# Decay rows through DRAM, side-by-side gate weights and one table load in a two-layer attention and delta-rule trunk

## The chip, the cores and the metric

One core of a Trainium2 chip runs the whole program. The metric is the device time of one execution, in microseconds; less is better. Four engines compute (TensorE, called PE in the profile, with its weight loads as PEld; VectorE, DVE; ScalarE, ACT; GpSimd, POOL), and SP only issues transfers.

## What is computed

A token sequence `x` of 256 by 2048 goes through two layers. Layer 0 is differential attention and a gated MLP with a short convolution (the FFN). Layer 1 is a gated delta rule (GDN) and the same kind of FFN. The change touches the beginning of layer 1 only:

```python
h = rms_norm(x, mixer_norm[1])
proj = h @ w_in                      # q, k, v, z and, last, b_gate and a_gate: 32 heads each
q, k, v = silu(causal_dwconv(...));  q, k = l2_norm(q), l2_norm(k)
beta = sigmoid(b_gate)
g = -exp(a_log) * softplus(a_gate + dt_bias)
g_c = cumsum(g)                      # within chunks of 64 in the reference
decay = exp(where(tril, g_c[:, None] - g_c[None, :], -inf))
low = where(strict, (k * beta) @ k.T * decay, 0);  qk = where(tril, q @ k.T * decay, 0)
```

So for every value head `h` the kernel needs a matrix whose element (i, j) depends on `g_c[i] - g_c[j]`: one of the two is a column (a scalar per partition), the other a row that must stand on all 128 partitions.

## The kernel before, in words

Activations live transposed: 128 features on partitions, 256 tokens along the row, in fp32 split into a high part (`fp32r`) and the rest. Every dense layer streams its weights. `weights()` (lines 78 to 91) loads one chunk `raw` of four 128-row blocks by 256 columns (512 KB) on SP's queue, ACT casts it to `whi` (line 89), and DVE subtracts for `wlo` (line 90). `dense()` (101) then makes three products per block and output tile, hi by hi, lo by hi, hi by lo (lines 115 to 117), 24 in a full chunk. `raw`, `whi` and `wlo` have three buffers each. After each chunk `tick()` (73) advances every generator in the list `bg` by one `yield`: all other work of a layer is written as such generators, and so is spread between the dense chunks.

This gives the program's order. The framework then orders each engine's instructions by a timeline that it simulates: what isn't ready there is passed by what is, and the result is fixed at build time. Each engine, and SP with its transfers, works through its own list in order.

In `gdn()` (409), the norm of layer 1 (`norm_stat`, 165) and the gates go first. `norm_stat` sums the squares by products with ones (177, 179), then `Ln` and `Exp` on ACT (182, 183). The gate weights are padded from 64 to 128 columns, and `dense` makes 16 x 3 products of them (664). `gates()` (704) scales the result (712), transposes it by two products with an identity (716), computes beta and the decays, their running sums by products with `triu` (744 to 752), and leaves a column tile `col` (negative sums by partition) and `rows`: 32 rows of sums in a high part and, 32 partitions below, the rest.

Then come four batches of four key heads. For each key head, `keys()` (455) makes for its two value heads a 128 x 128 matrix `sel` with ones in two rows (470, POOL, from the table `hot`), and a product of `sel` with `rows` (472) puts that head's row on all 128 partitions of a PSUM bank `gb`. DVE adds column and mask (475), ACT takes `Exp` (485 and 486, the latter from `gb` directly), in one block with the `Ln` and `Exp` of the l2 norm (480 to 482); a table set with both `ln` and `exp` is loaded for the block by `lnexp()` (189). SiLU (452) needs another table. PSUM has four `mp` banks for all such work. After the heads of a batch come its value heads, output gates `z` (dense_tok, 125) and, one batch later, the output products (`out`, 659), whose activations lie in the tile `oc`.

`HP`, `AP`, `OP`, `GAP` and `LEAD` (lines 23, 24) place the weight tiles in SBUF relative to the activations they meet, in elements modulo 128.

Of the kernel before, what the change touches and what calls it, by code (L numbers as in the profile page):

```python
# [3 lines left out]

# [12 lines left out]
P = 128  # L17
T = 256
# [9 lines left out]
class Trunk:  # L28
# [92 lines left out]
    def merge(self, ps, u):  # L121

        self.nc.vector.tensor_tensor(u, ps[:, :, :T], self.rstd.unsqueeze(1).to_broadcast([P, 2, T]), ALU.mult)  # L123

    def dense_tok(self, w, kt, acts):

        nc = self.nc
        ps = self.banks()
        for k0, nk in self.chunks(kt, CK // 2):
            hi, lo = self.weights(w[:, k0:k0 + nk, :], HP + LEAD)  # L130
            for k in range(nk):
                a = acts(k0 + k)
                first, last = k0 + k == 0, k0 + k == kt - 1
                for c in range(2):
                    ah, al = (a[:, i, c * P:(c + 1) * P] for i in range(2))
                    for j, (l, r) in enumerate(((ah, hi), (ah, lo), (al, hi))):
                        nc.tensor.matmul(ps[:, c, :], l, r[:, k, :], start=first and not j, stop=last and j == 2)  # L137
            self.tick()
        return ps
# [22 lines left out]
            nc.vector.tensor_tensor(self.ss, self.ss, sq, ALU.add)  # L162
        self.squares = []

    def norm_stat(self, wait=1):

        nc = self.nc
        r = self.sp.tile([P, T + 2], F32, tag="rstd", name="rstd", bufs=1)
        self.rstd, self.rstdc = r[:, :T], r[:, T:]
        for _ in range(wait):  # L170
            yield
        self.add_squares()
        yield
        self.add_squares()
        ss, self.ss = self.ss, None
        ps = self.mp()
        nc.tensor.matmul(ps[:, :T], self.ones, ss, start=True, stop=True)
        for c in range(2):
            nc.tensor.matmul(ps[:, T + c:T + c + 1], ss[:, c * P:(c + 1) * P], self.ones[:, :1], start=True, stop=True)
        m = self.sp.tile([P, T + 2], F32, tag="sq", name="ms", bufs=2)  # L180
        nc.vector.tensor_scalar(m, ps[:, :T + 2], 1.0 / D, EPS, ALU.mult, ALU.add)
        nc.scalar.activation(r, m, AF.Ln)
        nc.scalar.activation(r, r, AF.Exp, scale=-0.5)
        nc.vector.tensor_tensor(m, m, r, ALU.mult)
        nc.vector.tensor_tensor(m, m, r, ALU.mult)
        nc.vector.tensor_scalar(m, m, -0.5, 1.5, ALU.mult, ALU.add)
        nc.vector.tensor_tensor(r, r, m, ALU.mult)
# [218 lines left out]
            self.tick()  # L406
        return items[k]

    def gdn(self, w_gate, w_in, w_z, w_out, nb, hb, gate_ap, const_ap, hot_ap, conv_col, ng, done):

# [7 lines left out]
        gh = min(2, hb)  # L420
        gv = 2 * gh
        with tc.tile_pool(name="gd", bufs=1) as gd:
            self.spawn(self.norm_stat())
            con = gd.tile([P, 384], F32, tag="con", name="con")[:, :384]
            nc.sync.dma_start(con, const_ap)
            ident, mask, triu = con[:, :P], con[:, P:T], con[:, T:]
            hot = gd.tile([P, nv], F32, tag="hot", name="hot")
            nc.sync.dma_start(hot, hot_ap)
            gp = gd.tile([P, 2, nv], F32, tag="gp", name="gp")
            nc.sync.dma_start(gp, gate_ap)  # L430
            eps128 = gd.tile([P, 1], F32, tag="eps128", name="eps128")
# [23 lines left out]
            def keys(hq, c, cc, b0, res):  # L455
# [2 lines left out]
                nc.scalar.square(sq, c)  # L458
                sp = gd.tile([P, 2, 2, T], F32R, tag="qp", name="qp", bufs=1)
                self.split(sp, sq)  # L460
                yield
                yield
                while "rows" not in gates:
                    yield
                gb, gc = mp(), gates["col"]
                ds = []
                for v in range(2):
                    h = 2 * hq + v
                    sel = gd.tile([P, P], F32R, tag="sel", name="sel", bufs=2)
                    nc.gpsimd.tensor_copy(sel, hot[:, h:h + 1].to_broadcast([P, P]))  # L470
                    g = gb[:, v * T:(v + 1) * T]
                    nc.tensor.matmul(g, sel, gates["rows"], start=True, stop=True)
                    d = gd.tile([P, 384], F32, tag="d", name="d", bufs=2)
                    for t in range(2):
                        nc.vector.scalar_tensor_tensor(
                            d[:, (1 - t) * P:(2 - t) * P], g[:, t * P:(t + 1) * P], gc[:, t, h:h + 1], mask, ALU.add, ALU.add)
                    ds.append(d)
# [183 lines left out]
                    ps = self.dense(w_out[b * (KD // 2) + blk], 2 * hb, lambda k: self.await_(acts, k), OP)  # L661
                    self.add_out(blk, ps, done if b == nb - 1 else None)

            pg = self.dense(w_gate, KD, self.h_acts, HP, tiles=1)
            self.spawn(self.gates(gd, pg, nv, gp, ident, triu, gates))
            pend = None
            for b in range(nb):
                heads = range(b * hb, (b + 1) * hb)
# [32 lines left out]
                pend = (b, acts)  # L701
            out(*pend)

    def gates(self, gd, pg, nv, gp, ident, triu, res):

        nc, mp = self.nc, self.mp
        t0 = gd.tile([P, 4, 2, 64], F32, tag="vz", name="gt0", bufs=4)
# [5 lines left out]
        yield  # L713
        pt = mp()[:, :4 * nv].rearrange("p (t h) -> p t h", t=2)
        for t in range(2):
            nc.tensor.transpose(pt[:, t, :], lin[:2 * nv, t * P:(t + 1) * P], ident[:2 * nv, :2 * nv])
        for t in range(2):
            nc.vector.tensor_scalar(y[:, t, :nv], pt[:, t, :nv], -1.0, None, ALU.mult)
            nc.vector.tensor_tensor(y[:, t, nv:], pt[:, t, nv:], gp[:, 1, :], ALU.add)
# [10 lines left out]
        nc.vector.tensor_scalar(y, y, 0.0, None, ALU.max)  # L730
        nc.vector.scalar_tensor_tensor(q, q, 2.0, y, ALU.mult, ALU.add)
        a = gd.tile([P, nv], F32, tag="ga", name="ga")
        nc.scalar.activation(a, gp[:, 0, :], AF.Exp)
        if nv < 32:
            nc.vector.memset(w, 0.0)
        for t in range(2):
            for d in range(2):
                nc.vector.scalar_tensor_tensor(
                    w[:, t, 32 * d:32 * d + nv], q[:, t, nv:], -1.0, a, ALU.mult, ALU.mult)
        yield  # L740
        yield
        yield
# [3 lines left out]
        nc.tensor.matmul(pc[:, 1, :], self.ones, w[:, 0, :nv], start=False, stop=True)  # L746
        col = gd.tile([P, 2, nv], F32, tag="gc", name="gc")
        nc.vector.scalar_tensor_tensor(col, pc, -1.0, q[:, :, :nv], ALU.mult, ALU.subtract)
        pr = mp()[:64, :T]
        nc.tensor.matmul(pr[:, :P], w[:, 0, :], triu, start=True, stop=True)  # L750
        nc.tensor.matmul(pr[:, P:], w[:, 0, :], self.ones, start=True, stop=False)
        nc.tensor.matmul(pr[:, P:], w[:, 1, :], triu, start=False, stop=True)
        rows = gd.tile([P, T], F32R, tag="grow", name="grow")
        nc.gpsimd.memset(rows[64:].bitcast(F32), 0.0)
        nc.scalar.copy(rows[:64], pr)
        nc.vector.tensor_tensor(rows[32:64], pr[32:], rows[32:64].bitcast(F32), ALU.subtract)
        res["rows"], res["col"] = rows, col


NH = 8  # L760
# [11 lines left out]
def _layout(inputs):  # L772
# [30 lines left out]
    for t, n in ((0, P), (1, T)):  # L803
# [18 lines left out]
        "fcols1": fcols[1],  # L822
        "w_up0": blocks(x["ffn_w_up"][0], KD, up),
        "w_down0": blocks(x["ffn_w_down"][0], NJ, pairs(D // T)),
        "w_gate": np.pad(wi[:, 2 * kd + 2 * vd:], ((0, 0), (0, P - 2 * NV))).reshape(KD, P, P).transpose(1, 0, 2),
        "w_in": blocks(wi, KD, gin),
        "w_z": blocks(wi, KD, gz),
        "w_out": go.reshape(NB * (D // T), P, 2 * HB, T),
        "gate": np.broadcast_to(np.stack([x["gdn_A_log"][0], x["gdn_dt_bias"][0]]), (P, 2, NV)),
        "const": np.concatenate(const, 1).astype(f),  # L830
        "hot": np.concatenate([np.eye(NV)] * 2 + [np.zeros((P - 2 * NV, NV))]).astype(f),
        "w_up1": blocks(x["ffn_w_up"][1], KD, up),
        "w_down1": blocks(x["ffn_w_down"][1], NJ, pairs(D // T)),
    }
# [3 lines left out]
def trunk_kernel(tc, a, out):  # L838
    nc = tc.nc
    with ExitStack() as ctx:  # L840
        t = Trunk(ctx, tc)
        n = a["cols"].shape[1]
        cols = t.cp.tile([P, n], F32, tag="cols", name="cols")
        nc.sync.dma_start(cols[:, :KD], a["cols"][:, :KD])
        parts = t.chunks(KD, CK, 1)

        def load():
            if parts:
                k, n = parts.pop(0)
                nc.scalar.dma_start(t.x[:, k:k + n, :], a["x"][:, k:k + n, :])  # L850

        load()
        pos = [0]

        def take(n):
            pos[0] += n
            return cols[:, pos[0] - n:pos[0]]

        def one(c, i):
            return c[:, i:i + 1]  # L860

        mixer, ffn = take(2 * KD), take(2 * KD)
        qg, kg, lvec, sub, ng = take(1), take(1), take(4), take(2), take(1)
        gconv = take(4 * 4 * NQ)
        def then(gain, layer):
            return lambda k: t.norm_tile(k, one(gain, layer * KD + k))

        starts = [k for k, _ in parts]
        begun = []

        def start(k):

            if len(begun) <= k:
                if k == 0 or k in starts:
                    load()
                if k == KD - 1:
                    nc.scalar.dma_start(cols[:, KD:], a["cols"][:, KD:])
                then(mixer, 0)(k)
                t.add_squares()
                begun.append(k)  # L880
            return t.h[k]

        t.attention(a["w_qk"], a["w_v"], a["w_o"], NH, a["dist"], a["const"][:, :P], qg, kg, lvec, sub, start, then(ffn, 0),
                    0.8 - 0.6 * math.exp(-0.3 * 0))
        t.ffn(a["w_up0"], a["w_down0"], NJ, a["fcols0"], then(mixer, 1))
        t.gdn(a["w_gate"], a["w_in"], a["w_z"], a["w_out"], NB, HB, a["gate"], a["const"], a["hot"],
              lambda tap, tile_: one(gconv, tap * 4 * NQ + tile_), ng, then(ffn, 1))
        t.ffn(a["w_up1"], a["w_down1"], NJ, a["fcols1"],
              lambda k: nc.sync.dma_start(out[:, k, :], t.x[:, k, :]), final=True)
# [15 lines left out]
```

## Time and profile before

| | us |
|---|---|
| device time, median of 3 runs | 2651.64 |
| lowest and highest | 2649.69, 2652.61 |
| the profiled execution, device time | 2653.89 |
| its span in the profile | 2652.1 |
| TensorE, DVE, ACT, POOL busy in it | 2635.5, 1842.5, 1452.8, 110.9 |

Busy time of an engine is the time in which at least one of its instructions runs. Matmuls overlap, so their mean durations are latencies, and the distance between two starts is the pace. The granted TensorE clock is shown as a share of full speed (2.4 GHz; the other level is 1.2 GHz). The part of layer 1 before its FFN runs from about 1104 to 1910 us of the span.

### The profile page before, as it was taken

What the parts mean: (1) busy time and instruction counts of PE and PEld (TensorE: products, weight loads), DVE (VectorE), ACT (ScalarE), POOL (GpSimd) and SP (SyncE); (2) the same over time, 40 slices, a digit from 0 to 9 for tenths busy, and PEclk for the clock granted to TensorE, in tenths of its full rate; (3) what the DMA queues carried; (4) which work ended last, traced back from release to release, by engine and by line L of the source; (5) the groups of instructions that cost most, each with busy time, mean ns of one, the idle gap of its engine ahead of it and who ended that gap; (6) DMA issues with size and microseconds to landing.
All of it is one profiled execution on the core that took longest, in us unless ns stands there. A gap on an engine that the chain in (4) does not pass through costs nothing.

```text
span 2652.1 us, 53671 instructions
## 1 busy us (share of the span) xinstructions
PE 2635.5 (99%) x22352; PEld 2573.5 (97%) x22352; DVE 1842.5 (69%) x2719; ACT 1452.8 (55%) x1994; POOL 110.9 (4%) x221
## 2 busy tenths in 40 slices
PE   8999999999999999999999999999999999999999
PEld 8998899999999999999989989989999999999999
DVE  7776567777777555589788688688677777775444
ACT  6555555555555444485664674574555555554333
POOL 0000000000000000021011021021000000000000
PEclk9999999999999999999999999999999999999999
DMA  6555566666666666656455455555466666666665
GB/s 201 172 177 167 166 193 194 196 193 194 195 193 196 191 196 195 185 157 189 128 167 168 146 169 164 158 167 177 147 193 195 192 195 194 193 196 196 202 202 166
DMA packets 135460, 481.62 MB, mean 182 GB/s; under 512 B 15408, under 2 KB 18480, under 8 KB 135216
## 3 DMA queue, kind: packets, MB, share of 16 engines
q1 hardware_dynamic: 134064, 475.58, 60.1%
q8 instruction: 175, 2.87, 0.5%
q10 hardware_dynamic: 1152, 2.61, 0.3%
q14 instruction: 69, 0.57, 0.1%
HBM read 476.03 MB, written 2.10 MB: 180 GB/s over the span
## 4 chain that ended last, share of the span: by engine, by line
PE 96%; ACT 2%; DVE 2%; issue 1%; DMA 0%; SPq 0%; DVEq 0%; ACTq 0%
PE ps L116 27%; PE ps L115 27%; PE ps L117 27%; PE ps L137 10%; PE mp L607 2%; PE mp L223 1%; DVE wlo L90 0%; ACT whi L89 0%; PE mp L495 0%; PE mp L577 0%; PE mp L571 0%; DVE cv L204 0%; PE mp L586 0%; DMA raw<-w_qk 0%; PE mp L651 0%
## 5 line engine op out<-in xcount | busy, mean ns | idle before, releaser
L90 DVE TENSOR_TENSOR wlo<-raw,whi 128x1024 fp32r<-128x1024 f32 (+2 forms) x909 | 1105.9, 1218 | 638.8 <-ACT whi L89 636.8
L89 ACT CAST whi<-raw 128x1024 fp32r<-128x1024 f32 (+2 forms) x909 | 948.2, 1044 | 1011.8 <-PE ps L117 839.4
L115 PE MATMUL ps<-h,whi 128*128 128x256 f32 x4304 | 1193.6, 278 | 8.9 <-ACT h L149 5.6
L116 PE MATMUL ps<-h,wlo 128*128 128x256 f32 x4304 | 1194.0, 277 | 3.1 <-DVE wlo L90 3.1
L117 PE MATMUL ps<-h,whi 128*128 128x256 f32 x4304 | 1192.7, 277 | 0.0
L115 PEld LDWEIGHTS ps<-h,whi 128*128 128x128 f32 x4304 | 809.8, 188 | 11.0 <-ACT h L149 5.6
L116 PEld LDWEIGHTS ps<-h,wlo 128*128 128x128 f32 x4304 | 810.5, 188 | 6.1 <-DVE wlo L90 4.0
L117 PEld LDWEIGHTS ps<-h,whi 128*128 128x128 f32 x4304 | 810.4, 188 | 0.5
L115 PE MATMUL ps<-ac,whi 128*128 128x256 f32 x1632 | 450.4, 276 | 0.0
L116 PE MATMUL ps<-ac,wlo 128*128 128x256 f32 x1632 | 450.3, 276 | 0.0
L117 PE MATMUL ps<-ac,whi 128*128 128x256 f32 x1632 | 450.2, 276 | 0.0
L116 PEld LDWEIGHTS ps<-ac,wlo 128*128 128x128 f32 x1632 | 306.3, 188 | 0.0
L115 PEld LDWEIGHTS ps<-ac,whi 128*128 128x128 f32 x1632 | 306.3, 188 | 0.0
L117 PEld LDWEIGHTS ps<-ac,whi 128*128 128x128 f32 x1632 | 306.2, 188 | 0.0
L137 PE MATMUL ps<-whi,h 128*128 128x512 f32 x768 | 240.8, 390 | 0.0
L137 PEld LDWEIGHTS ps<-whi,h 128*128 128x128 f32 x768 | 144.1, 188 | 29.8
L137 PE MATMUL ps<-wlo,h 128*128 128x512 f32 x384 | 149.9, 390 | 0.1
L115 PE MATMUL ps<-oc,whi 128*128 128x256 f32 x512 | 143.1, 280 | 0.0
L204 DVE SCALAR_TENSOR_TENSOR cv<-u,fcols,cv 128x255 f32<-128x255 f32 (+1 forms) x344 | 142.9, 478 | 0.0
L117 PE MATMUL ps<-oc,whi 128*128 128x256 f32 x512 | 142.8, 279 | 0.0
L116 PE MATMUL ps<-oc,wlo 128*128 128x256 f32 x512 | 142.8, 279 | 0.0
L123 DVE TENSOR_TENSOR u<-ps,rstd 128x512 f32<-128x512 f32 x118 | 81.5, 690 | 38.7 <-PE ps L117 38.3
(200 smaller groups left out, 2037.9 us busy)
## 6 DMA issues: line engine op xcount, KB each, us to landing
raw<-w_up SPq DMA_DIRECT2D x344, 512.0 KB, 4.3
raw<-w_down SPq DMA_DIRECT2D x160, 512.0 KB, 4.1
raw<-w_in SPq DMA_DIRECT2D x128, 512.0 KB, 4.2
raw<-w_z SPq DMA_DIRECT2D x64, 512.0 KB, 3.9
raw<-w_out SPq DMA_DIRECT2D x64, 512.0 KB, 3.9
raw<-w_qk SPq DMA_DIRECT2D x63, 512.0 KB, 4.1
raw<-w_v SPq DMA_DIRECT2D x32, 512.0 KB, 3.7
raw<-w_o SPq DMA_DIRECT2D x32, 512.0 KB, 4.2
```

The costliest lines, as they stand in the source:

```text
L89: nc.scalar.copy(hi, raw)
L90: nc.vector.tensor_tensor(lo, raw, hi.bitcast(F32), ALU.subtract)
L115: nc.tensor.matmul(o, hi[:, k, s], a[:, 0, :], start=first, stop=False)
L116: nc.tensor.matmul(o, lo[:, k, s], a[:, 0, :], start=False, stop=False)
L117: nc.tensor.matmul(o, hi[:, k, s], a[:, 1, :], start=False, stop=last)
L123: self.nc.vector.tensor_tensor(u, ps[:, :, :T], self.rstd.unsqueeze(1).to_broadcast([P, 2, T]), ALU.mult)
L137: nc.tensor.matmul(ps[:, c, :], l, r[:, k, :], start=first and not j, stop=last and j == 2)
L204: nc.vector.scalar_tensor_tensor(out[:, j:], u[:, :T - j], taps[n - 1 - j], out[:, j:], ALU.mult, ALU.add)
L223: last = self.nc.tensor.matmul(out, self.onesr, p[:, j], start=i + j == 0, stop=i + j == n)
L607: nc.tensor.matmul(p[:, v, :], l(v), r[:, v, :], start=i == 0, stop=i == len(terms) - 1)
```

## The change

The three parts are independent.

1. The decay rows go to a DRAM tile `decays` once, in plain fp32. Each key head reads its two rows back by one transfer with a stride of zero over the partitions, into an SBUF tile `gb` of 128 x 512 with one buffer. `sel`, its product and the high/low form of `rows` go.
2. The gate weights are no longer padded; `dense_gate` keeps the high part and the rest of 64 columns side by side in one 128-column tile. One product of all 128 columns with the high part of `h`, and one of the 64 high columns with the rest of `h`, replace three. The transposing products in `gates` take a table `fold` (two 64 x 64 identities one above the other) in place of the identity, and so add the two halves.
3. In the GDN's first norm, `Ln` and `Exp` run behind one load of the common table set, and the gates' `Exp` of `a_log` is kept behind them.

```diff
+    def dense_gate(self, w, kt):
+        nc = self.nc
+        ps = self.banks()
+        n = w.shape[2]
+        for k0, nk in self.chunks(kt, CK):
+            raw = self.wp.tile([P, CK * T], F32, tag="raw", name="raw", bufs=3)
+            raw = raw[:, :nk * n].rearrange("p (k n) -> p k n", n=n)
+            both = self.wp.tile([P, CK * T + P], F32R, tag="whi", name="whi", bufs=3)
+            d = (HP - GAP) % P
+            both = both[:, d:d + nk * 2 * n].rearrange("p (k i n) -> p k i n", i=2, n=n)
+            nc.sync.dma_start(raw, w[:, k0:k0 + nk, :])
+            nc.scalar.copy(both[:, :, 0, :], raw)
+            nc.vector.tensor_tensor(both[:, :, 1, :], raw, both[:, :, 0, :].bitcast(F32), ALU.subtract)
+            for k in range(nk):
+                a = self.h[k0 + k]
+                passes = [(2 * n, both[:, k].rearrange("p i n -> p (i n)"), a[:, 0, :]), (n, both[:, k, 0, :], a[:, 1, :])]
+                for m, l, r in passes if k0 + k == 0 else passes[::-1]:
+                    nc.tensor.matmul(ps[:m, 0, :T], l, r, start=k0 + k == 0 and m > n, stop=k0 + k == kt - 1 and m > n)
+            self.tick()
+        return ps
...
-        nc.scalar.activation(r, m, AF.Ln)
-        nc.scalar.activation(r, r, AF.Exp, scale=-0.5)
+        with self.lnexp(last) if switch else nullcontext():
+            nc.scalar.activation(r, m, AF.Ln)
+            self.rexp = nc.scalar.activation(r, r, AF.Exp, scale=-0.5)
...
-            hot = gd.tile([P, nv], F32, tag="hot", name="hot")
-            nc.sync.dma_start(hot, hot_ap)
+            fold = gd.tile([P, 2 * nv], F32, tag="fold", name="fold")
+            nc.sync.dma_start(fold, fold_ap)
+            decays = tc.dram_tile([nv, T], F32, name="decays")
...
-                yield
-                yield
-                while "rows" not in gates:
+                while "col" not in gates:
                     yield
-                gb, gc = mp(), gates["col"]
+                gb, gc = gd.tile([P, 2 * T], F32, tag="gb", name="gb", bufs=1), gates["col"]
+                nc.sync.dma_start(gb.rearrange("p (v t) -> p v t", v=2),
+                                  decays[2 * hq:2 * hq + 2, :].unsqueeze(0).to_broadcast([P, 2, T]))
+                yield
+                yield
...
-                    sel = gd.tile([P, P], F32R, tag="sel", name="sel", bufs=2)
-                    nc.gpsimd.tensor_copy(sel, hot[:, h:h + 1].to_broadcast([P, P]))
                     g = gb[:, v * T:(v + 1) * T]
-                    nc.tensor.matmul(g, sel, gates["rows"], start=True, stop=True)
...
-            pg = self.dense(w_gate, KD, self.h_acts, HP, tiles=1)
+            pg = self.dense_gate(w_gate, KD)
...
-            nc.tensor.transpose(pt[:, t, :], lin[:2 * nv, t * P:(t + 1) * P], ident[:2 * nv, :2 * nv])
+            nc.tensor.matmul(pt[:, t, :], lin[:4 * nv, t * P:(t + 1) * P], fold[:4 * nv, :], start=True, stop=True)
...
-        nc.scalar.activation(a, gp[:, 0, :], AF.Exp)
+        with self.tc.issue_after(self.rexp.ins):
+            nc.scalar.activation(a, gp[:, 0, :], AF.Exp)
         for t in range(2):
-            for d in range(2):
-                nc.vector.scalar_tensor_tensor(
-                    w[:, t, 32 * d:32 * d + nv], q[:, t, nv:], -1.0, a, ALU.mult, ALU.mult)
+            nc.vector.scalar_tensor_tensor(w[:, t, :nv], q[:, t, nv:], -1.0, a, ALU.mult, ALU.mult)
...
-        rows = gd.tile([P, T], F32R, tag="grow", name="grow")
-        nc.gpsimd.memset(rows[64:].bitcast(F32), 0.0)
-        nc.scalar.copy(rows[:64], pr)
-        nc.vector.tensor_tensor(rows[32:64], pr[32:], rows[32:64].bitcast(F32), ALU.subtract)
-        res["rows"], res["col"] = rows, col
+        rows = gd.tile([nv, T], F32, tag="grow", name="grow")
+        nc.scalar.copy(rows, pr)
+        nc.sync.dma_start(decays, rows)
+        res["col"] = col
```

The three products with `triu` and ones that make `pr` keep their number, with 32 stationary columns in place of 64.

## Rows read from the trace of the kernel before

**Rows 1.** The page: span, TensorE's line of part 1, line of part 4

```profile
span 2652.1 us, 53671 instructions
...
PE 2635.5 (99%) x22352; PEld 2573.5 (97%) x22352; DVE 1842.5 (69%) x2719; ACT 1452.8 (55%) x1994; POOL 110.9 (4%) x221
...
PE 96%; ACT 2%; DVE 2%; issue 1%; DMA 0%; SPq 0%; DVEq 0%; ACTq 0%
```

**Rows 2.** Windows: length, busy of PE, PEld, DVE, ACT, POOL (starts), PEclk, DMA

```profile
1050.00:1100.00 50.00, 50.00 (x444) 50.00 (x443) 24.67 (x24) 20.19 (x23) 0.00 (x0) 1.00 0.63 184
...
1150.00:1200.00 50.00, 49.81 (x324) 44.95 (x323) 42.78 (x73) 43.09 (x65) 19.67 (x38) 1.00 0.53 157
```

**Rows 3.** Windows of 5 us behind the gate weights

```profile
1115.00:1120.00 5.00, 3.87 (x27) 3.27 (x27) 4.52 (x10) 3.14 (x4) 0.00 (x0) 0.96 0.47 161
1120.00:1125.00 5.00, 5.00 (x34) 5.00 (x33) 4.42 (x10) 1.36 (x2) 0.00 (x0) 0.70 0.75 231
```

**Rows 4.** Chain that ended last, in order of time: start us, us, what

```profile
1105.83 4.75 DMA raw<-w_in
...
1111.75 1.28 ACT L182
...
1115.20 0.95 ACT whi L89
1116.17 1.23 DVE wlo L90
```

**Rows 5.** Timeline of TensorE: start us, us, engine, line, what, count, idle before

```profile
1104.26 0.28 PE L115 MATMUL ps<-h,whi 128*128 128x256 f32 x1
...
1108.47 0.59 PE L177 MATMUL mp<-ss,ones 128*128 128x256 f32 x2
...
1109.27 0.36 PE L116 MATMUL ps<-h,wlo 128*128 128x256 f32 x1
...
1116.19 0.38 PE L115 MATMUL ps<-h,whi 128*128 128x256 f32 x1
1117.45 0.39 PE L116 MATMUL ps<-h,wlo 128*128 128x256 f32 x1 [0.88 <-DVE wlo L90]
```

**Rows 6.** TensorE groups, 1100 to 1920 us: count, busy us, mean ns, idle

```profile
L472 PE MATMUL mp<-grow,sel 128*128 128x256 f32 x32 | 11.1, 348 | 0.0
```

**Rows 7.** The page, part 6: transfers, their size, us to landing

```profile
raw<-w_in SPq DMA_DIRECT2D x128, 512.0 KB, 4.2
...
raw<-w_gate SPq DMA_DIRECT2D x4, 256.0 KB, 3.0
```

**Rows 8.** Who waited for whom: us in total, times, longest

```profile
ACT whi L89 <- DMA raw<-w_in: 10.6, 8, 2.9
```

**Rows 9.** Timelines of ACT and DVE around the second key head

```profile
1152.23 0.36 ACT L486 ACTIVATE d<-mp,gc 128x128 f32<-128x128 f32 x1
...
1160.27 0.60 DVE L475 SCALAR_TENSOR_TENSOR d<-mp,gc,con 128x128 f32<-128x128 f32 x2
```

**Rows 10.** Timeline of DVE: the second gate chunk

```profile
1103.07 0.69 DVE L90 TENSOR_TENSOR wlo<-raw,whi 128x512 fp32r<-128x512 f32 x1 [2.03 <-ACT whi L89]
```

**Rows 11.** Timeline of SP's queue

```profile
1103.79 0.33 SPq L88 DMA_DIRECT2D raw<-w_in  x1
1104.45 0.33 SPq L425 DMA_DIRECT2D con<-const  x1
```

**Rows 12.** Timeline of ACT: the norm's table loads

```profile
1108.94 1.28 ACT L733 ACT_TABLE_LOAD   x1
...
1113.48 1.28 ACT L183 ACT_TABLE_LOAD   x1
1114.78 0.42 ACT L183 ACTIVATE rstd<-rstd 128x258 f32<-128x258 f32 x1
```

**Rows 13.** The page, part 5: dense products on `ac` and on `oc`

```profile
L115 PE MATMUL ps<-ac,whi 128*128 128x256 f32 x1632 | 450.4, 276 | 0.0
...
L115 PE MATMUL ps<-oc,whi 128*128 128x256 f32 x512 | 143.1, 280 | 0.0
```

More of the change, by code (lines that the diff above doesn't have):

```diff
@@ L2 @@
 from collections import deque
-from contextlib import ExitStack
+from contextlib import ExitStack, nullcontext
 import concourse.bass as bass
@@ L163, in add_squares, with norm_stat @@
         self.squares = []
-    def norm_stat(self, wait=1):
+    def norm_stat(self, wait=1, switch=False):
         nc = self.nc
@@ L178, in norm_stat @@
         for c in range(2):
-            nc.tensor.matmul(ps[:, T + c:T + c + 1], ss[:, c * P:(c + 1) * P], self.ones[:, :1], start=True, stop=True)
+            last = nc.tensor.matmul(
+                ps[:, T + c:T + c + 1], ss[:, c * P:(c + 1) * P], self.ones[:, :1], start=True, stop=True)
         m = self.sp.tile([P, T + 2], F32, tag="sq", name="ms", bufs=2)
         nc.vector.tensor_scalar(m, ps[:, :T + 2], 1.0 / D, EPS, ALU.mult, ALU.add)
-        nc.scalar.activation(r, m, AF.Ln)
-        nc.scalar.activation(r, r, AF.Exp, scale=-0.5)
+        with self.lnexp(last) if switch else nullcontext():
+            nc.scalar.activation(r, m, AF.Ln)
+            self.rexp = nc.scalar.activation(r, r, AF.Exp, scale=-0.5)
         nc.vector.tensor_tensor(m, m, r, ALU.mult)
@@ L407, in await_, with gdn @@
         return items[k]
-    def gdn(self, w_gate, w_in, w_z, w_out, nb, hb, gate_ap, const_ap, hot_ap, conv_col, ng, done):
+    def gdn(self, w_gate, w_in, w_z, w_out, nb, hb, gate_ap, const_ap, fold_ap, conv_col, ng, done):
         nc, tc, mp = self.nc, self.tc, self.mp
@@ L422, in gdn @@
         with tc.tile_pool(name="gd", bufs=1) as gd:
-            self.spawn(self.norm_stat())
+            self.spawn(self.norm_stat(switch=True))
             con = gd.tile([P, 384], F32, tag="con", name="con")[:, :384]
@@ L662, in out @@
                     self.add_out(blk, ps, done if b == nb - 1 else None)
-            pg = self.dense(w_gate, KD, self.h_acts, HP, tiles=1)
-            self.spawn(self.gates(gd, pg, nv, gp, ident, triu, gates))
+            pg = self.dense_gate(w_gate, KD)
+            self.spawn(self.gates(gd, pg, nv, gp, fold, triu, decays, gates))
             pend = None
@@ L702, in gdn, with gates @@
             out(*pend)
-    def gates(self, gd, pg, nv, gp, ident, triu, res):
+    def gates(self, gd, pg, nv, gp, fold, triu, decays, res):
         nc, mp = self.nc, self.mp
@@ L732, in gates @@
         a = gd.tile([P, nv], F32, tag="ga", name="ga")
-        nc.scalar.activation(a, gp[:, 0, :], AF.Exp)
-        if nv < 32:
-            nc.vector.memset(w, 0.0)
+        with self.tc.issue_after(self.rexp.ins):
+            nc.scalar.activation(a, gp[:, 0, :], AF.Exp)
         for t in range(2):
-            for d in range(2):
-                nc.vector.scalar_tensor_tensor(
-                    w[:, t, 32 * d:32 * d + nv], q[:, t, nv:], -1.0, a, ALU.mult, ALU.mult)
+            nc.vector.scalar_tensor_tensor(w[:, t, :nv], q[:, t, nv:], -1.0, a, ALU.mult, ALU.mult)
         yield
@@ L748, in gates @@
         nc.vector.scalar_tensor_tensor(col, pc, -1.0, q[:, :, :nv], ALU.mult, ALU.subtract)
[L749 to L752, printed above, removed]
-        rows = gd.tile([P, T], F32R, tag="grow", name="grow")
-        nc.gpsimd.memset(rows[64:].bitcast(F32), 0.0)
-        nc.scalar.copy(rows[:64], pr)
-        nc.vector.tensor_tensor(rows[32:64], pr[32:], rows[32:64].bitcast(F32), ALU.subtract)
-        res["rows"], res["col"] = rows, col
+        pr = mp()[:nv, :T]
+        nc.tensor.matmul(pr[:, :P], w[:, 0, :nv], triu, start=True, stop=True)
+        nc.tensor.matmul(pr[:, P:], w[:, 0, :nv], self.ones, start=True, stop=False)
+        nc.tensor.matmul(pr[:, P:], w[:, 1, :nv], triu, start=False, stop=True)
+        rows = gd.tile([nv, T], F32, tag="grow", name="grow")
+        nc.scalar.copy(rows, pr)
+        nc.sync.dma_start(decays, rows)
+        res["col"] = col
 NH = 8
@@ L824, in _layout @@
         "w_down0": blocks(x["ffn_w_down"][0], NJ, pairs(D // T)),
-        "w_gate": np.pad(wi[:, 2 * kd + 2 * vd:], ((0, 0), (0, P - 2 * NV))).reshape(KD, P, P).transpose(1, 0, 2),
+        "w_gate": wi[:, 2 * kd + 2 * vd:].reshape(KD, P, 2 * NV).transpose(1, 0, 2),
         "w_in": blocks(wi, KD, gin),
@@ L830, in _layout @@
         "const": np.concatenate(const, 1).astype(f),
-        "hot": np.concatenate([np.eye(NV)] * 2 + [np.zeros((P - 2 * NV, NV))]).astype(f),
+        "fold": np.concatenate([np.eye(2 * NV)] * 2).astype(f),
         "w_up1": blocks(x["ffn_w_up"][1], KD, up),
@@ L885, in trunk_kernel @@
         t.ffn(a["w_up0"], a["w_down0"], NJ, a["fcols0"], then(mixer, 1))
-        t.gdn(a["w_gate"], a["w_in"], a["w_z"], a["w_out"], NB, HB, a["gate"], a["const"], a["hot"],
+        t.gdn(a["w_gate"], a["w_in"], a["w_z"], a["w_out"], NB, HB, a["gate"], a["const"], a["fold"],
               lambda tap, tile_: one(gconv, tap * 4 * NQ + tile_), ng, then(ffn, 1))
```

## The prediction, made before the changed kernel was run

> **What bounds the kernel now.** I read the page first: TensorE is busy for 2635.5 of 2652.1 us, and the chain that ended last is TensorE for 96% [rows 1]. So a product that is taken away is time, wherever TensorE isn't kept waiting by something else. Then the windows, for the pace. In a window of the FFN, 50 us hold 444 product starts, 0.1126 us each; in the first stretch of the key heads TensorE is still busy for 49.8 of 50 us, but DVE and ACT are busy for 43 us each, so there all three are near their limits [rows 2]. The 280 ns that the page gives for one product is its latency, since products overlap; what a removed one is worth is the 0.1126 us.
>
> One place stands out, the first chunks after the gate weights. The 5 us windows from 1115 and 1120 hold 27 and 34 starts where 44.4 is the pace, and in the second the granted clock is 0.70, some of it therefore at the lower level of 1.2 GHz [rows 3]. (44.4 - 27) + (44.4 - 34) = 27.8 starts, 3.1 us; some 0.3 us of that is the gates' two small products, so about 2.8 us are lost. The chain in order of time says why: a weight transfer, a table load on ACT, ACT's cast at 1115.20, DVE's subtraction at 1116.17 [rows 4]. TensorE began the third chunk at 1116.19, and its second product, which needs that subtraction, at 1117.45 [rows 5]: 1.15 us of standing still beyond the pace. The clock fell only after that.
>
> **Part 1, the spread rows.** Removed: 32 products of `sel` with the rows [rows 6], 32 copies on POOL, one PSUM bank held per head. 32 x 0.1126 = 3.6 us of TensorE. Bounds: the mean latency in this group is 348 ns against some 280 of its neighbours, so if that excess of 70 ns goes as well it is 32 x 0.18 = 5.8 us; if the heads in which DVE and ACT are the late ones give nothing back (I count up to half), 1.8 us. I take 3.6, because TensorE's idle share of 0.2 us in 50 [rows 2] says it is seldom the one that waits.
>
> Added: one write of the rows to DRAM and 16 reads of 256 KB, all on SP's queue, which also issues every weight transfer. 256 KB of gate weights land in 3.0 us, 512 KB of `w_in` in 4.2 [rows 7], so a read in front of a weight transfer delays it by about 1.2 us. That matters only where a cast waits for its transfer: 8 of the 128 `w_in` casts did [rows 8]. 16 x 8/128 x 1.2 = 1.2 us; a waiting cast is not yet a waiting TensorE, so I take half, 0.6 us. Bounds: nothing, and 16 x 1.2 = 19 us if every one got through.
>
> The read's own latency: `gb` has one buffer, so head i+1's read waits for head i's last `Exp` on it. For the first head that ended at 1152.6, and the next head's first use of its row began at 1160.27 [rows 9]: 7.7 us for a transfer that should land in 3.0 to 4.2. Hidden there; in heads that follow closer, DVE waits for it. DVE then loses its lead in subtracting weights, and TensorE is next. For the first head, rows go to DRAM and back, two transfers in series, some 6 to 8 us later than by product; the dense products behind it don't need it.
>
> The smaller edits (POOL's clearing of the rows, DVE's subtraction of their second half, two of four writes of `w`) lie on engines with idle time at that point, some 0.2 to 0.4 us each: nothing. `fold` makes the two transposes ordinary products of 64 columns, as before: nothing.
>
> **Part 2, the gate weights.** 48 products become 32: 16 x 0.1126 = 1.8 us of TensorE. The weights of a chunk halve; DVE's subtraction took 0.69 us for 512 columns and 1.23 for 1024 [rows 4, 10], so 0.42 us for 256 by that line. But TensorE then comes sooner to the first chunk of the first key head, and that chunk comes by its own route. The gate products started at 1104.26, stopped at 1108.47 for the norm's and resumed at 1109.27 [rows 5], 0.8 us; 32 products and 0.8 end at 1108.7. The transfer of the first `w_in` chunk was issued at 1103.79 [rows 11], behind the second gate chunk's subtraction; that ends some 0.5 us earlier now: 1103.3, then 4.2 to land [rows 7], 0.95 for the cast and 1.23 to subtract [rows 4]: 1109.7. TensorE waits 1.0 us. The second chunk's transfer stays at 1105.83 with its 4.75 us [rows 4], behind the three small tables: 1110.6 + 0.95 + 1.23 = 1112.8, against 1112.4 for TensorE (a chunk is 24 products, 2.7 us). So little of the 1.8 us is seen here by itself; it is seen if the third chunk is ready.
>
> **Part 3, one table load.** Three loads of 1.28 us stand on ACT before the third chunk's cast, at 1108.94, 1111.75 and 1113.48 [rows 4, 12]. One stays. The first lay partly in a wait for a transfer, so between 1.3 and 2.6 us come off the chain: the cast starts at 1112.6 to 1113.9 in place of 1115.20, and the chunk is ready at 1114.8 to 1116.1. TensorE reaches it at 1115.5. Against 1117.45 that is 1.3 to 1.9 us; if the clock then stays up, the other 1.6 us of the loss go too: 2.9 to 3.5. If two waits of 1.0 and 0.4 us bring the clock down again, only the first sum stays. I take 3.2 us for parts 2 and 3 together, bounds 1.3 and 4.6 (all of 2.8 and 1.8).
>
> What a load costs is read here from its row: the load at 1113.48 ended at 1114.76 and the `Exp` started at 1114.78, 0.02 us on [rows 12]. The Trainium skill (ScalarE: Activation LUTs, What ACT_TABLE_LOAD costs) adds a drain of 1380 ns to each load of 1283 ns. By that, two loads would be worth 5.3 us of ACT, and the sum above would reach its bound of 4.6; the row shows the load and no drain.
>
> **A side effect.** The tiles of the `gd` pool move: `fold` takes 128 bytes per partition more than `hot`, `gb` 1024 more than `sel`. The tile `oc` so moves by 128 bytes modulo the 512 for which `OP` and `GAP` place the weights against it. The trace has no product at the new distance. The nearest rows are the mean latencies at the old one, 276 ns for `ac` and 280 for `oc` [rows 13]: 4 ns of spread without any change. 512 x 3 products x 4 ns = 6 us either way. I take nothing, as both rows stand at one distance and the spread may be the other work beside them.
>
> **Sum.** -3.6 + 0.6 - 3.2 = -6.2 us. The profiled execution took 2653.9 us (span 2652.1); 2647.7 by the sum. It lies 2.3 us over the median of the runs, 2651.6, which gives **2645.4 us** for the median. 0.2% is 5.3 us, about what a measurement of this kernel can tell from no change: the line is at 2646.3, close by.
>
> **Rivals.** *(a) The dip stays.* TensorE waits for the first and second chunk in place of the third, and the clock falls once more: parts 2 and 3 give 1.3, the sum is -4.3: 2647.3, no change that can be told. For it: the waits of 1.0 and 0.4 us worked out above are no shorter than the one that came before the dip.
> *(b) The key heads loosen.* With both rows of a head there at once and a PSUM bank free, ACT and DVE stop waiting in the heads, and the 70 ns per removed product come back too: 3.6 becomes 5.8, the dip is gone wholly (4.6): -9.8: 2641.8. For it: 43 us busy on both engines [rows 2]. Against: TensorE idles so little there that there is not much to give back.
> *(c) `oc` is worse placed*: +6, so 2651.4, no change; better placed, 2639. For it: the constants that set the old distance are left as they are; against: no row shows a distance at work.
> *(d) Slower: SP stands still.* The read for head i+1 waits at the head of SP's queue for head i's last `Exp`; the weight transfers behind it can't be issued. If it stood where the program has it, after the first chunk of the next head's weights, the next chunk would start from that `Exp`: ACT's work (a table load of 1.28 us [rows 12] and seven activations of some 0.36 [rows 9], 3.8 us), 4.2 + 0.95 + 1.23 for the weights, then two chunks of 2.7 up to the next such work: 15.6 us for a head of four chunks, 10.8. 12 heads follow another: 12 x 4.8 = +58 us, 2703. It decides as soon as the read is queued over 2 us before its buffer is free. Against: the queue isn't in program order. The program has `con` before all gate weights; SP issued it at 1104.45, after the first `w_in` chunk [rows 11], as its buffer became free. A scheduler that does that will not queue a read long before its buffer is free.
> The Trainium skill (DMA: Bandwidth & Descriptors, Anatomy of one DMA) speaks for (d): a semaphore wait happens on the issuing sequencer before dispatch. The trace has SP waiting for buffers, but issuing `con` 0.7 us after the transfer before it [rows 11].
>
> **Chances.** The forecast 0.50 (two thirds of it under 2646.3), (a) 0.20, (b) 0.14, (c) 0.09, mostly no change, (d) 0.07. Faster 0.34 + 0.14 + 0.02 = 0.50; slower 0.07 + 0.03 = 0.10; the same 0.40. The range, 2641 to 2651.5, takes in (a), (b) and nearly all of (c), and leaves out (d) and the far ends.
>
> **What would show it.** Right: no row for `sel`; TensorE products fewer by 48; one table load between 1104 and 1116; the 5 us windows there at 44 starts from the third chunk on; `oc` products still at 280 ns; SP's waits for `gb` all under 2 us. Wrong: ACT or DVE waiting for `gb` by 1 us or more in most heads; a wait of SP on ACT with TensorE idle behind it; a clock under 1.0 around 1110.

## The result, and the profile after

The changed kernel takes **2657.8 us** (median of 12 runs, 2656.4 to 2659.6) where the kernel before takes 2651.2 (12 runs): 1.0024 of its time, 95% interval 1.0016 to 1.0032. That is 6.6 us slower; 2645.4 had been forecast, and the range ended at 2651.5.

The page of the changed kernel, the lines that answer to [rows 1] and [rows 13]:

```profile
span 2655.2 us, 53535 instructions
...
PE 2639.0 (99%) x22306; PEld 2576.5 (97%) x22306; DVE 1839.9 (69%) x2716; ACT 1442.6 (54%) x1986; POOL 94.9 (4%) x188
...
PE 97%; ACT 1%; DVE 1%; DMA 0%; issue 0%; SPq 0%; DVEq 0%; ACTq 0%
...
L115 PE MATMUL ps<-ac,whi 128*128 128x256 f32 x1632 | 450.6, 276 | 0.0
...
L115 PE MATMUL ps<-oc,whi 128*128 128x256 f32 x512 | 146.3, 286 | 0.0
```

TensorE has fewer products and is busy for longer. Two lines say where to look: the products on `ac` stand at 276 ns as before, those on `oc`, the output layer of the delta rule, went from 280 to 286.

How much that is, the ends of the output blocks show: after each, DVE adds the block to `x`. Two neighbouring blocks of the last batch, where TensorE runs nothing else, first in the kernel before and then in the changed one (timeline of DVE):

```profile
1918.38 0.69 DVE L229 TENSOR_TENSOR x<-ps,x 128x512 f32<-128x512 f32 x1 [0.28 <-PE ps L117]
1923.82 0.69 DVE L229 TENSOR_TENSOR x<-ps,x 128x512 f32<-128x512 f32 x1 [0.28 <-PE ps L117]
```

```profile
1919.13 0.69 DVE L253 TENSOR_TENSOR x<-ps,x 128x512 f32<-128x512 f32 x1 [0.65 <-PE ps L117]
1925.05 0.69 DVE L253 TENSOR_TENSOR x<-ps,x 128x512 f32<-128x512 f32 x1 [0.65 <-PE ps L117]
```

A block of 48 products takes 5.92 us in place of 5.44: 0.1233 us a start against 0.1133. TensorE is busy without a break there in both kernels, at a granted clock of 1.00.

Everywhere else the change did about what had been worked out. One table load is left in the first norm, answering to [rows 12], and the windows that answer to [rows 3] hold 37, 40 and then 47 starts (timeline of ACT, then windows, both of the changed kernel):

```profile
1108.61 1.05 ACT L89 CAST whi<-raw 128x1024 fp32r<-128x1024 f32 x1 [2.46 <-DMA raw<-w_in]
1109.68 1.28 ACT L215 ACT_TABLE_LOAD   x1
1110.98 0.42 ACT L206 ACTIVATE rstd<-ms 128x258 f32<-128x258 f32 x1
1111.30 1.03 ACT L89 CAST whi<-raw 128x1024 fp32r<-128x1024 f32 x1
```

```profile
1105.00:1110.00 5.00, 4.63 (x37) 4.35 (x37) 2.32 (x5) 2.42 (x3) 0.80 (x1) 1.00 0.85 277
1110.00:1115.00 5.00, 4.51 (x40) 4.32 (x39) 3.56 (x5) 4.18 (x7) 0.00 (x0) 1.00 0.53 161
1115.00:1120.00 5.00, 5.00 (x47) 5.00 (x46) 4.35 (x12) 1.83 (x3) 0.00 (x0) 1.00 0.82 256
```

SP does wait for the buffer of the 16 reads, 34.6 us in 19 waits, the longest 4.4; the reads land in 3.1 to 5.2 us, and DVE waited for one of them once (SP's own waits, then the view of the tile `gb`):

```profile
SPq L489 <- DVE d L499: 21.3, 9, 4.4
SPq L489 <- ACT d L510: 9.5, 6, 3.3
SPq L489 <- ACT d L509: 3.8, 4, 1.4
```

```profile
  DVE d L499: 2.7, 1
...
DMA to landing us min/median/max: 3.1/3.6/5.2
```

So there were two theories: **P**, the output weights stand badly against `oc`, which has moved; and **S**, the reads hold up SP, DVE or ACT. A distance is the start of the activations less the start of the weights, in elements modulo 128. No trace shows an address: 45 is the kernel's constant `GAP`, and the moves follow from the sizes of the tiles.

### The profile page after: what moved, and what is told of

Read it like the earlier page. It is cut to its first block, busy times and chain, and to the rows that moved or that the text cites. A ratio compares the mean times of both kernels' runs of the same rounds, so it can differ in the third digit from the quotient of the medians.

```text
span 2655.2 us, 53535 instructions
## 1 busy us (share of the span) xinstructions
PE 2639.0 (99%) x22306; PEld 2576.5 (97%) x22306; DVE 1839.9 (69%) x2716; ACT 1442.6 (54%) x1986; POOL 94.9 (4%) x188
## 4 chain that ended last, share of the span: by engine, by line
PE 97%; ACT 1%; DVE 1%; DMA 0%; issue 0%; SPq 0%; DVEq 0%; ACTq 0%
PE ps L116 27%; PE ps L117 27%; PE ps L115 27%; PE ps L159 10%; PE mp L631 2%; PE mp L247 1%; PE mp L519 0%; PE mp L601 0%; PE mp L595 0%; ACT whi L89 0%; PE mp L610 0%; DVE wlo L90 0%; PE mp L675 0%; PE mp L364 0%; PE mp L394 0%; DMA raw<-w_qk 0%
## 5 line engine op out<-in xcount | busy, mean ns | idle before, releaser
L90 DVE TENSOR_TENSOR wlo<-raw,whi 128x1024 fp32r<-128x1024 f32 (+1 forms) x905 | 1102.1, 1219 | 646.9 <-ACT whi L89 645.1
L89 ACT CAST whi<-raw 128x1024 fp32r<-128x1024 f32 (+1 forms) x905 | 945.8, 1046 | 1025.6 <-PE ps L117 847.7
L115 PE MATMUL ps<-h,whi 128*128 128x256 f32 x4288 | 1188.7, 278 | 7.8 <-ACT h L171 5.8
L115 PEld LDWEIGHTS ps<-h,whi 128*128 128x128 f32 x4288 | 806.1, 188 | 9.6 <-ACT h L171 5.8
L115 PE MATMUL ps<-ac,whi 128*128 128x256 f32 x1632 | 450.6, 276 | 0.0
L115 PEld LDWEIGHTS ps<-ac,whi 128*128 128x128 f32 x1632 | 306.4, 188 | 0.0
L115 PE MATMUL ps<-oc,whi 128*128 128x256 f32 x512 | 146.3, 286 | 0.0
L117 PE MATMUL ps<-oc,whi 128*128 128x256 f32 x512 | 146.1, 286 | 0.0
```

What stands on the lines that cost most here:

```text
L89: nc.scalar.copy(hi, raw)
L90: nc.vector.tensor_tensor(lo, raw, hi.bitcast(F32), ALU.subtract)
L115: nc.tensor.matmul(o, hi[:, k, s], a[:, 0, :], start=first, stop=False)
L117: nc.tensor.matmul(o, hi[:, k, s], a[:, 1, :], start=False, stop=last)
```

## The experiments

**The distance put right, and put wrong.** `OP` sets where a weight tile starts: `OP - GAP`, modulo 128 elements (512 bytes). `oc` lay at 112 and lies at 16 in the changed kernel, so its weights stood 45 elements before it and now stand 77.

```diff
-HP, AP, OP = 40, 48, 112
+HP, AP, OP = 40, 48, 16
```

> The changed kernel with OP = 16 in place of 112, so that the output weights stand again 45 elements (modulo 128) before the tile oc, which has moved by 32. Theory P, placement: the 1536 output products run at 0.123 us a start because their weights stand 77 elements off; the eight last output blocks take 5.44 us again in place of 5.92, 32 blocks x 0.48 = 15.4 us come back: 2642.4 us (2640.5 to 2645). Rival S, the reads through SP and DVE's and ACT's waits for them cost the time: 2657.8 as before, and the output blocks still at 5.9.

Measured: **2645.8 us**, 0.9979 (0.9970 to 0.9989) of the kernel before, 12.0 us under the changed kernel. The block is back at 5.44 us (timeline of DVE):

```profile
1909.56 0.69 DVE L253 TENSOR_TENSOR x<-ps,x 128x512 f32<-128x512 f32 x1 [0.30 <-PE ps L117]
1915.00 0.69 DVE L253 TENSOR_TENSOR x<-ps,x 128x512 f32<-128x512 f32 x1 [0.29 <-PE ps L117]
```

The same constant in the kernel before, with no other edit:

```diff
-HP, AP, OP = 40, 48, 112
+HP, AP, OP = 40, 48, 80
```

> The kernel before with OP = 80 in place of 112 and nothing else, so that its output weights stand 77 elements off, as in the changed kernel. Theory P: 2651.2 + 15.4 = 2666.6 us, output blocks of 5.92 us. Rival S (the reads are the cause): 2651.2, blocks of 5.44.

Measured: 2662.1 us, 1.0040 (1.0028 to 1.0053): 10.7 us more, without a single read through DRAM. The page of this run has the changed kernel's line again:

```profile
L115 PE MATMUL ps<-oc,whi 128*128 128x256 f32 x512 | 146.1, 286 | 0.0
```

S is out as the cause of the loss. Both expectations were 3 to 5 us off in size: 0.48 us a block holds in the last batch; in the three earlier ones the starts on `oc` lie at 0.120 to 0.121 us against 0.114 to 0.115, so the 32 blocks lose some 11 us and not 15.4.

Is it the distance, or where `oc` lies? Unused elements behind an earlier table bring every later tile back to its old place:

```diff
-            con = gd.tile([P, 384], F32, tag="con", name="con")[:, :384]
+            con = gd.tile([P, 384 + 96], F32, tag="con", name="con")[:, :384]
```

> The changed kernel with OP = 112 and 96 unused elements behind the table con, so that oc and all tiles behind fold stand where they stood modulo 128. If the distance between weights and oc is what counts: 2642.4 us, as with OP = 16. If the address of either alone counts: somewhere between 2642 and 2657.8. Rival S: 2657.8.

Measured: 2646.8 us, 0.9982 (0.9973 to 0.9991), and 279 ns for the products on `oc`. `oc` at 16 with `OP` 16 and `oc` at 112 with `OP` 112 agree within the spread, and `oc` at 16 with `OP` 112 and at 112 with `OP` 80 both run at 285 to 286 ns: the distance counts, and not where either lies. In the next two runs `oc` lies at 80 and at 48, again at a distance of 45, and its products take 279 to 280 ns.

**Each part alone, at the right distance.** The rows through DRAM, with the padded gate weights and the old norm:

> The kernel before with the first part alone (rows through DRAM, no sel product) and OP = 80, which keeps the output weights 45 elements before oc (oc lies at 80 here). The prediction's terms for it: -3.6 for the 32 products, +0.6 for the reads: 2648.4 us (2647 to 2650). Rival: the reads hold up SP in the heads, 2651 or more; then SP waits on d's readers with TensorE idle behind them.

Measured: 2648.7 us, 0.9991 (0.9982 to 0.9999). 2.4 us gained where 3.0 were expected.

The gate weights alone:

> The kernel before with the second part alone (gate weights side by side, fold) and OP = 48, which keeps the distance of 45 (oc lies at 48 here). TensorE has 1.8 us less to do, but the third chunk's cast still stands behind three table loads: 2650.5 to 2651.4. Rival: the 1.8 us come through: 2649.6.

Measured: 2650.7 us, 0.9998 (0.9989 to 1.0007): nothing that can be told, as expected as long as the third chunk stands behind three table loads.

The one table load alone:

> The kernel before with the third part alone: Ln and Exp of the first delta-rule norm behind one table load, the gates' Exp behind them. The prediction's working for this part: the third chunk's cast starts 1.3 to 2.6 us sooner and the dip behind it goes: 2648.2 to 2649.9. Rival: two loads are hidden behind a transfer, and the time stays at 2651.2.

Measured: 2653.5 us, 1.0007 (0.9998 to 1.0016), a miss: no gain, rather a loss. In the first norm the part does what it should: every window from 1105 to 1130 shows TensorE without an idle stretch, such as this one:

```profile
1115.00:1120.00 5.00, 5.00 (x44) 4.81 (x44) 4.53 (x11) 2.00 (x3) 0.00 (x0) 1.00 0.73 212
```

But the scheduler has ordered the key heads anew, and in the third batch TensorE now stands still for longer and the clock falls after it. Windows of this kernel there, and then of the kernel before:

```profile
1545.00:1550.00 5.00, 3.13 (x12) 2.10 (x11) 3.45 (x5) 4.99 (x11) 0.99 (x3) 0.91 0.23 84
1550.00:1555.00 5.00, 5.00 (x21) 4.17 (x20) 4.57 (x10) 2.95 (x6) 0.00 (x0) 0.74 0.76 220
```

```profile
1545.00:1550.00 5.00, 4.63 (x35) 4.45 (x36) 2.99 (x4) 4.94 (x8) 0.00 (x0) 1.00 0.61 164
1550.00:1555.00 5.00, 5.00 (x23) 4.06 (x22) 5.00 (x10) 2.78 (x5) 3.78 (x9) 1.00 0.47 153
```

ACT is busy for 4.99 and 4.94 of 5 us: at this place it is the late one, and whether TensorE has work left seems to hang on the order of its list (no run shows that by itself). The fall of the clock isn't the whole loss: five of the eleven runs had a mean granted clock of 1.000 and still took 2652.7 us in the middle, where the kernel before takes 2650.9 at that clock. (The lower counts in the second window are the 512-column products of `z`.)

The other way round, the changed kernel with `OP` = 16 and without the third part:

```diff
-            self.spawn(self.norm_stat(switch=True))
+            self.spawn(self.norm_stat())
...
-        with self.tc.issue_after(self.rexp.ins):
-            nc.scalar.activation(a, gp[:, 0, :], AF.Exp)
+        nc.scalar.activation(a, gp[:, 0, :], AF.Exp)
```

> The changed kernel with OP = 16 and without the third part (three table loads in the first norm again). If the third part is worth what the prediction gave it, 1.3 to 3.2 us: 2647.1 to 2649. If it only moves the schedule about, as alone it gave 2.1 us away with a new standstill in the third batch: within 1 us of 2645.8 or under.

Measured: 2649.9 us, 0.9993 (0.9984 to 1.0002), 4.1 us over the same kernel with the part, and above both expectations. The clock has a share in that: 6 of these 11 runs have a mean granted clock of 0.999, and 1 of 10 with the part; in the runs at 1.000 the difference is 2.6 us. With the shorter gate phase in front, the two loads stand right before the third chunk (ACT's timeline, and the windows):

```profile
1109.59 1.28 ACT L206 ACT_TABLE_LOAD   x1
1111.33 1.28 ACT L207 ACT_TABLE_LOAD   x1
```

```profile
1110.00:1115.00 5.00, 3.55 (x27) 2.96 (x25) 2.68 (x4) 4.92 (x7) 0.00 (x0) 1.00 0.50 170
1115.00:1120.00 5.00, 4.71 (x41) 4.71 (x42) 4.59 (x13) 2.22 (x3) 0.00 (x0) 1.00 0.65 191
```

TensorE stands idle there for 1.45 + 0.29 us, and the windows hold 27 and 41 starts where 44 would go. So part 3 pays where the gate phase is short: the gate weights alone gained 0.4 us, the load alone lost 2.1 (not certainly), the gate weights on top of part 1 lost 1.2 (2648.7 to 2649.9), and both on top of part 1 gained 2.9 (2648.7 to 2645.8). Parts 1 and 3 without 2 were not run, so that part 3 needs part 2 is likely and not shown.

**How sharp the distance is.** First the kernel before with `OP` = 16, a distance of 13:

> The kernel before with OP = 16: output weights 13 elements before oc in place of 45. Output products start every 0.1136 to 0.1149 us at 45 and 0.120 to 0.123 at 77. If 45 lies in a wide good stretch: 0.114 here, 2651; if it is a narrow optimum: 0.118 or more, 2657 or more.

Measured: 2662.4 us (one run), and the same 286, 285 and 285 ns in the three lines as at 77. Then the changed kernel with both `AP` (products on `ac`) and `OP` (on `oc`) set anew, one run each:

```diff
-HP, AP, OP = 40, 48, 112
+HP, AP, OP = 40, 32, 32
```

> The changed kernel with AP = 32 and OP = 32: the weights of the products on ac stand 61 elements before it, those on oc 29 (45 for both before). What has been seen: 0.1133 us a start at 45 (ac, oc, h), 0.120 to 0.123 at 13 and 77 (oc). If what counts is that 45 is far enough from both 0 and some other distance, 29 and 61 run at 0.113 as well; if the optimum is narrow, each of them at 0.116 to 0.123, so up to 1632 x 3 x 0.008 = 39 us more for ac, and 2646 to 2700 us in all.

```diff
+HP, AP, OP = 40, 56, 8
```

> The changed kernel with AP = 56 and OP = 8: distances of 37 (ac) and 53 (oc). By a wide good stretch both run at 0.113; by a narrow optimum at 45 both are at 0.115 or more. Time 2646 to 2670 us.

```diff
+HP, AP, OP = 40, 112, 61
```

> The changed kernel with AP = 112 and OP = 61: distances of 109 (ac) and 0 (oc). The slow level is expected for both, 0.120 to 0.123: 2646 + 1632 x 3 x 0.008 + 11 = 2696 us. If the pattern repeats every 64 elements, 109 is as good as 45: ac at 0.113 and 2657 us.

```diff
+HP, AP, OP = 40, 44, 20
```

> The changed kernel with AP = 44 and OP = 20: distances of 49 (ac) and 41 (oc), four elements to either side of 45. Seen so far, us a start: 45 and 109 at 0.113, 61 at 0.116, 53 at 0.118, 37 at 0.119. If the good stretch is wide enough for layouts that are off by a few elements, 0.113 to 0.114 for both and 2646 us; if it is narrower than 8 elements, 0.115 or more for one or both: 2650 to 2665 us.

Measured: 2668.8, 2686.3, 2654.4 and 2684.4 us. One window of 50 us in layer 0's FFN, in its down projection, where only products on `ac` run, in the kernel before (45 elements) and in these four in turn (61, 37, 109 and 49 elements):

```profile
950.00:1000.00 50.00, 50.00 (x444) 50.00 (x443) 26.58 (x30) 22.36 (x27) 0.00 (x0) 1.00 0.68 195
```

```profile
950.00:1000.00 50.00, 50.00 (x431) 50.00 (x431) 26.12 (x29) 21.47 (x27) 0.00 (x0) 1.00 0.61 188
```

```profile
950.00:1000.00 50.00, 50.00 (x419) 50.00 (x418) 23.82 (x24) 19.45 (x23) 0.00 (x0) 1.00 0.59 184
```

```profile
950.00:1000.00 50.00, 50.00 (x444) 50.00 (x443) 26.57 (x29) 22.39 (x27) 0.00 (x0) 1.00 0.63 196
```

```profile
950.00:1000.00 50.00, 50.00 (x421) 50.00 (x420) 25.28 (x27) 21.09 (x27) 0.00 (x0) 1.00 0.60 184
```

So 45 and 109 give 0.1126 us a start, 61 gives 0.1160, 49 0.1188 and 37 0.1193. On `oc` the mean latencies are 278 to 280 ns at 45; 282 to 283 at 29 and 53; 283 to 284 at 41; 285 at 0; 285 to 286 at 13 and 77 (the line of L115 at 45, 29, 53, 41 and 0, in this order):

```profile
L115 PE MATMUL ps<-oc,whi 128*128 128x256 f32 x512 | 142.7, 279 | 0.0
L115 PE MATMUL ps<-oc,whi 128*128 128x256 f32 x512 | 144.3, 282 | 0.0
L115 PE MATMUL ps<-oc,whi 128*128 128x256 f32 x512 | 144.8, 283 | 0.0
L115 PE MATMUL ps<-oc,whi 128*128 128x256 f32 x512 | 145.3, 284 | 0.0
L115 PE MATMUL ps<-oc,whi 128*128 128x256 f32 x512 | 145.8, 285 | 0.0
```

The times agree: at 49, 1632 x 3 x 0.0062 = 30 us for `ac` and 1536 x 0.005 = 8 for `oc`, on 2645.8: 2684, measured 2684.4. At 37 and 53 the guess of at most 2670 us was too low by 16 us, and at 49 and 41 that of at most 2665 by 19: a narrow optimum had been allowed for, but not priced at 5 to 6%. At 109 the slow pace was expected and the good one came; of the two times given for it, 2696 and 2657 us, the second, with a period of 64 elements, was the right one.

## Why the prediction was wrong

- **The step that failed is "A side effect".** It had the tile, the 128 bytes and the modulus, and then put the price at nothing, with bounds of 6 us either way from the latencies 276 and 280 ns. Both rows stand at a distance of 45, so their spread says nothing of what another distance costs; the step said as much and still used it as an end of the range. Measured: 10.7 us in the kernel before, 12.0 in the changed one. Rival (c) was this mechanism, with half its size and a chance of 0.09.
- **Part 1** was forecast at -3.6 + 0.6 = -3.0 and measured at -2.4 alone. The 32 products went, the reads landed as estimated (3.6 us in the middle, against 3.0 to 4.2). The two terms aren't shown one by one: from 1130 to 1910 us TensorE stands idle for 0.9 us in the kernel before, for 3.5 with part 1 alone and for 2.4 in the changed kernel, more than the 0.6 allowed for the reads. That SP's waits would all stay under 2 us was wrong, the longest is 4.4. By the prediction's own limit of 2 us, rival (d) should then have come, and it did not: in the key heads of the changed kernel no standstill of TensorE is longer than 0.8 us.
- **Parts 2 and 3** were forecast at -3.2 together and measured at -2.9 together, on top of part 1. That the 1.8 us of the gate products show only when the third chunk is ready fits: alone they gave 0.4. Rival (a) did not come: TensorE does wait for the subtractions of the first two chunks, 0.24 and 0.49 us, and the clock stays at 1.00.
- **The dip** was counted as a fixed loss. In the kernel with `OP` = 80, which is the same up to the output products, TensorE stood still in the same place, and the granted clock stayed at 1.00 (windows):

```profile
1115.00:1120.00 5.00, 3.90 (x30) 3.55 (x30) 4.83 (x11) 1.64 (x2) 0.00 (x0) 1.00 0.48 134
1120.00:1125.00 5.00, 5.00 (x44) 5.00 (x43) 4.72 (x10) 3.11 (x5) 0.00 (x0) 1.00 0.74 225
```

  So the drop to 0.70 [rows 3] belongs to some executions and not to all. The times say the same: of the 26 runs of the kernel before that go with the first experiments, 15 had a mean granted clock of 1.000 and took 2650.9 us in the middle, 11 had 0.999 and took 2652.6; where the clock fell, only the profiled one shows. So some 1.6 us of the 3.2 weren't there to be had in every run, and the step of 2.3 us from the profiled execution down to the median had very likely taken them off already. That 2.9 us came out all the same is luck in part: part 2 on top of part 1 lost 1.2 us, and part 3 then gave 4.1.
- **The sum without the side effect** was 2645.4 us; with the distance put right the changed kernel takes 2645.8. The gains came out 0.6 and 0.3 us smaller than forecast, and the median from which the sum started was some 0.5 us high, so the agreement is closer than the terms. This version, one constant away from the change, is faster than both: 0.9979 of the kernel before.

## What to carry to other kernels

Whoever adds, drops or resizes a tile in a pool moves all that lies behind it: compute the new address of every operand that stands in the dense products, and set the constants that depend on it in the same edit. An operand whose placement has been tuned is a cost with no row in the trace of before; where a change moves it, one run with the constant set to a bad distance prices it, and until then it deserves a wide bound and a rival of full size. And parts that shift one engine's list should be tried together and one by one: here two of them are worth little or nothing alone and 2.9 us together, on top of the first.

## What the runs showed of the hardware

The pace of back-to-back products of 256 `fp32r` columns depends on where the stationary weights lie relative to the moving activations within a partition. Over eleven distances it is best at 45 and 109 elements (0.1126 us on `ac`) and alike at 13 and 77 (285 to 286 ns on `oc`, and 2662 us in the kernel before), so the pattern fits a period of 64 elements (256 bytes). The 128 bytes by which `oc` moved are half of that; by the same pattern a move by 256 bytes would cost nothing. Within the period the good place is narrow, since 4 elements to either side already cost 5% (on `ac`, at 49) or most of what 13 and 77 cost (on `oc`, at 41). In the five windows on `ac` the granted clock is 1.00, and DVE, ACT and the transfers have time to spare.

The Trainium skill (TensorE: Matmul & The Clock Gate, Step-by-step: what each phase is for) says that TensorE reads the streaming operand and the next weights by two independent ports of SBUF, so that loading weights takes no read bandwidth from the running matmul. It says nothing of placement, and from it alone one would expect placement to be worth nothing. The runs here show otherwise, 444 against 419 to 431 starts in 50 us by the placement alone; what it is that collides, and whether it is the load of the weights, no run here shows.
